# HGRN2 recurrence: near levels formed by groups of 32 tokens instead of whole blocks of 128

## The chip, the core and the metric

One Trainium2 chip, one core. The kernel computes a whole decoder layer in one launch, and the metric is its device time in microseconds (us). The tensor engine is called PE, its weight loads PEld, the vector engine DVE, the scalar engine ACT, GpSimd POOL; SP and ACT issue the DMAs.

## What is computed

A layer of width 2048 over 256 tokens: RMSNorm, one wide projection, two token mixers (block attention, and a gated linear recurrence), two gates that merge them, an output projection, and an MLP of 2048 to 8192 to 2048. The part that the change touches is the recurrence, with 8 heads, keys and values of 128:

```python
f = lb + (1 - lb) * sigmoid(f_pre);  k = 1 - f;  q = silu(q)
S_t = diag(f_t) S_{t-1} + k_t v_t^T          # state, 128 x 128 a head
o_t = S_t^T q_t
```

Unrolled, `o_t` is a sum over `s <= t` of `score[s, t] * v_s`, where `score[s, t]` sums over the 128 key dimensions `k_s * f_{s+1} * ... * f_t * q_t`. For `s = t` no decay stands between them.

## The kernel before

**The weight stream.** All products with weights go through "units" of 128x2048 float32, 1 MB each, loaded by SP in order (`load`), cut into two float32r parts, `hi` on ACT (line 116) and `lo` on DVE (line 117), two units ahead of their use (`cut`, `unit`, three buffers each of `raw`, `hi` and `lo`). A projection unit makes one 128x256 slice of the result: 16 products with `hi` and a moving operand of 512 columns (line 283, high and low part of the activation at once), and 16 with `lo` and 256 columns (line 285). The result leaves PSUM by ACT and DVE (`summed`, lines 296 and 297). Four PSUM banks hold such results.

**The work at the side.** Recurrence and attention are generators. After each unit, `step()` runs up to two of them for a budget of some us; each `yield` names an estimated cost. So PE's order is: one unit, a short burst of small products, the next unit, and so on. `recur(g, q, f)` handles four heads, for g = 0 and 1; it is started after the eight units that make its q and f.

**Scores by levels.** `recur` makes `score[s, t]` in a tile `sd` of 128 x 8 x 128: source token s on the partitions, 8 pairs of head h and block t of 128 tokens, target token in the row. The diagonal (line 339) is `ks^T q`, of which line 340 keeps the diagonal by a predicated copy with the mask `cmt`. Then level lv, with `h2 = 2**lv`, covers the pairs in which s lies in the left half and t in the right half of one group of `2*h2` tokens. The tiles `ks` and `qp` hold the decayed keys and queries for that level; DVE multiplies the next factors into them after each level (lines 392 to 395). For levels 0 to 4 one product a pair of head and block (line 361) takes all 128 keys as weights and the 64 right-half queries as the moving operand. It computes 128 x 64 scores, of which the mask keeps those inside a group (line 376). Levels 5 and 6 compute only what is needed, with weights of 32 or 64 keys (line 369): at level 5 the outputs go to partitions 0 to 31 and 64 to 95, at level 6 to partitions 0 to 63. ACT copies them to `sd` (line 384). Level 7 joins the two blocks (line 400). Lines 411 to 413 multiply the scores by the values.

These products are plain float32, and the trace shows two records for each, called passes here: level 5 has 16 products and 32 passes a burst; a level of 0 to 4, and the diagonal, 8 products and 16 passes.

**Constants.** `load_consts` issues three DMAs on SP after the fourth unit: `cft`, `rope` and `cmt`.

Of the kernel before, what the change touches and what calls it, by code (L numbers as in the profile page):

```python
# [11 lines left out]
I32 = mybir.dt.int32  # L12
AF = mybir.ActivationFunctionType
# [3 lines left out]
P = 128  # L17
# [13 lines left out]
def layer_kernel(ctx: ExitStack, tc: tile.TileContext, xT, vecs, wv, wm, wg, wu, wo, w1, w2, cf, cm, out):  # L31
    nc = tc.nc

    cp = ctx.enter_context(tc.tile_pool(name="const", bufs=1))
# [9 lines left out]
    def uid(s):  # L44
        cnt[0] += 1
        return f"{s}_{cnt[0]}"

    def g4(s, shape=(P, 1024), dt=F32):
        return gp.tile(list(shape), dt, tag="g", name=uid(s))

    def s1(s, dt=F32, n=256):
        return sp.tile([P, n], dt, tag=f"s{n}", name=uid(s), bufs=6 if n == 256 else 3)

    def bank(s, pool=pp):
        return pool.tile([P, 512], F32, tag="b", name=uid(s))
# [107 lines left out]
        load(u)  # L163
    cft = cp.tile([P, 128 + 256], F32, name="cft")
    rope = cp.tile([32, 512], F32, name="rope")
    cmt = cp.tile([P, 128 + 5 * 64], I32, name="cmt")

    def load_consts():
        nc.sync.dma_start(cft, cf[:, :384])
        nc.sync.dma_start(rope, cf[:32, 384:896])  # L170
        nc.sync.dma_start(cmt, cm)

    ident = cft[:, :128]
    cmask = cft[:, 128:384]
# [81 lines left out]
    for c in range(4):  # L256
        pst = [bank(f"pv{t}", pm) for t in range(2)]
        for q in range(4):
            hi, lo = unit()
            hi, lo = (x.rearrange("p (k f) -> p k f", k=4) for x in (hi, lo))  # L260
            for k in range(4):
                kk = 4 * q + k
                for t in range(2):
                    xh = xcat[:, kk, t * P : (t + 1) * P]
                    xl = xcat[:, kk, T + t * P : T + (t + 1) * P]
                    nc.tensor.matmul(pst[t], xh, hi[:, k, :], start=(kk == 0), stop=False)  # L266
                    nc.tensor.matmul(pst[t], xh, lo[:, k, :], start=False, stop=False)  # L267
                    nc.tensor.matmul(pst[t], xl, hi[:, k, :], start=False, stop=(kk == KD - 1))  # L268
            if c == 0 and q == 3:
                load_consts()  # L270
                side.append(prepare())
            step(3.6)
            if q == 3 and full:
                leave(*full.pop())
        full.append((c, pst))
# [42 lines left out]
    def recur(g, q, f):  # L318
        sg = g4("rsg", (P, 4, T))
        nc.scalar.activation(sg, q, AF.Sigmoid)  # L320
        nc.scalar.activation(f, f, AF.Sigmoid)
        nc.vector.tensor_mul(q, q, sg)
        yield 1.2
        for h in range(4):
            hh = 4 * g + h
            nc.vector.tensor_scalar(
                f[:, h, :], f[:, h, :], lb[:, 1, hh : hh + 1], lb[:, 0, hh : hh + 1], op0=OP.mult, op1=OP.add
            )
        ks = g4("rks", (P, 4, T))
        nc.vector.tensor_scalar(ks, f, -1.0, 1.0, op0=OP.mult, op1=OP.add)  # L330
        sd = g4("rsd", (P, 8, P))
        nc.gpsimd.memset(sd, 0.0)
        yield 1.5
        for b in range(2):
            pd = bank("pd")
            for i in range(4):
                h, t = divmod(4 * b + i, 2)
                c = slice(t * P, (t + 1) * P)
                nc.tensor.matmul(pd[:, i * P : (i + 1) * P], ks[:, h, c], q[:, h, c], start=True, stop=True)  # L339
            nc.vector.copy_predicated(  # L340
                sd[:, 4 * b : 4 * b + 4, :],
                cmt[:, None, :128].to_broadcast([P, 4, P]),
                pd.rearrange("p (a t) -> p a t", a=4),
            )
        qp = g4("rqp", (P, 4, T))
        nc.vector.tensor_mul(qp, q, f)
        yield 2.3
        sx = g4("rsx", (P, 4, P))
        tot = f.rearrange("p h t -> p (h t)")
        for lv in range(LEVELS):  # L350
            h2 = 1 << lv
            nb = P // (2 * h2)
            pd = bank("pd")
            if lv < 7:
                for h in range(4):
                    for t in range(2):
                        i = 2 * h + t
                        if lv < 5:
                            c = slice(t * P, (t + 1) * P)
                            rhs = qp[:, h, c].rearrange("p (n a j) -> p n a j", a=2, j=h2)[:, :, 1, :]  # L360
                            nc.tensor.matmul(  # L361
                                pd[:, i * 64 : (i + 1) * 64].rearrange("p (n j) -> p n j", j=h2),
                                ks[:, h, c], rhs, start=True, stop=True,
                            )
                            continue
                        for n in range(nb):
                            at = n * 2 * h2
                            c = t * P + at
                            nc.tensor.matmul(  # L369
                                pd[at : at + h2, i * h2 : (i + 1) * h2],  # L370
                                ks[:, h, c : c + h2], qp[:, h, c + h2 : c + 2 * h2], start=True, stop=True,
                            )
                if lv < 5:
                    mk = cmt[:, 128 + 64 * lv : 192 + 64 * lv].rearrange("p (n j) -> p n j", j=h2)
                    dst = sd.rearrange("p i (n a j) -> p i n a j", a=2, j=h2)[:, :, :, 1, :]
                    nc.vector.copy_predicated(
                        dst,
                        mk[:, None, :, :].to_broadcast([P, 8, nb, h2]),
                        pd.rearrange("p (i n j) -> p i n j", i=8, j=h2),
                    )  # L380
                else:
                    for n in range(nb):
                        at = n * 2 * h2
                        nc.scalar.activation(
                            sd[at : at + h2, :, at + h2 : at + 2 * h2],
                            pd[at : at + h2, : 8 * h2].rearrange("p (i j) -> p i j", i=8), AF.Copy,
                        )
                kv = ks.rearrange("p h (n a j) -> p (h n) a j", a=2, j=h2)
                qv = qp.rearrange("p h (n a j) -> p (h n) a j", a=2, j=h2)
                tv = tot.rearrange("p (n a) -> p n a", a=2)  # L390
                n = kv.shape[1]
                nc.vector.tensor_mul(kv[:, :, 0, :], kv[:, :, 0, :], tv[:, :, 1:2].to_broadcast([P, n, h2]))
                nc.vector.tensor_mul(qv[:, :, 1, :], qv[:, :, 1, :], tv[:, :, 0:1].to_broadcast([P, n, h2]))
                nt = sp.tile([P, n], F32, tag="tot" if n > 256 else "tots", name=uid("tot"), bufs=2)
                nc.vector.tensor_mul(nt, tv[:, :, 0], tv[:, :, 1])
                tot = nt
                yield 2.2
            else:
                for h in range(4):
                    nc.tensor.matmul(  # L400
                        pd[:, h * P : (h + 1) * P], ks[:, h, :P], qp[:, h, P:], start=True, stop=True
                    )
                nc.scalar.activation(sx, pd.rearrange("p (h t) -> p h t", h=4), AF.Copy)
                yield 0.1
        o = g4("ro", (P, 4, T))
        for b in range(2):
            po = bank("po")
            for j in range(2):
                h = 2 * b + j
                hc = slice((4 * g + h) * P, (4 * g + h + 1) * P)  # L410
                nc.tensor.matmul(po[:, j * T : j * T + P], ii[0][:, hc], sd[:, 2 * h, :], start=True, stop=True)
                nc.tensor.matmul(po[:, j * T + P : (j + 1) * T], ii[0][:, hc], sx[:, h, :], start=True, stop=False)
                nc.tensor.matmul(
                    po[:, j * T + P : (j + 1) * T], ii[1][:, hc], sd[:, 2 * h + 1, :], start=False, stop=True
                )
            nc.scalar.activation(o[:, 2 * b : 2 * b + 2, :], po.rearrange("p (h t) -> p h t", h=2), AF.Copy)
        ro[g] = o
        yield 0.1
# [111 lines left out]
    for g in range(2):  # L530
        q = g4("rq", (P, 4, T))
# [13 lines left out]
    for g in range(2):  # L545
        q = g4("aq", (P, 4, T))
# [17 lines left out]
    for j in range(KD):  # L564
# [8 lines left out]
        r = s1("r")  # L573
        summed(pr, r)
        nc.vector.tensor_mul(r, r, gr)
        a = s1("a")
# [10 lines left out]
    for c in range(4):  # L587
        t = g4("x2", (P, 4, T))
# [36 lines left out]
    for part in range(4):  # L625
        ucat = []
        for j in range(16):
# [5 lines left out]
            t = s1("t")  # L633
# [115 lines left out]
```

## Time and profile before

| what | us |
|---|---|
| median of 3 runs | 1441.9 (1441.51 to 1443.44) |
| profiled execution, its own time | 1443.69 |
| its span, first to last instruction | 1441.9 |
| PE busy in the span | 1435.0 |
| DVE, ACT, POOL busy | 881.5, 695.2, 4.4 |

The profile shows one execution. Busy times are shares of the span; an idle engine that nothing waits for costs nothing. What an edit is worth is read from the stage in which it lies.

### The profile page before, as it was taken

To read this page: it belongs to the slowest core of one execution; us is meant where nothing else is said; L and a number is where in the kernel's file an instruction comes from. 1 tells how busy PE (TensorE), PEld (TensorE's weight loads), DVE (VectorE), ACT (ScalarE), POOL (GpSimd) and SP (SyncE) were. 2 spreads that over 40 slices of the span, in tenths; PEclk is the share of its full clock that TensorE was granted. 3 is DMA by queue.
4 is the path that set the end of the run, shared out by engine and by line. 5 is a ranking of instruction groups with operands and counts; after the bars stand their busy time and mean duration, and the time that the engine had idled before them with its cause. 6 is when DMAs were issued, how large, how long until landed. Compare 5 with 4: busy or idle time off the path is not lost.

```text
span 1441.9 us, 18721 instructions
## 1 busy us (share of the span) xinstructions
PE 1435.0 (100%) x7824; PEld 1244.3 (86%) x7824; DVE 881.5 (61%) x958; ACT 695.2 (48%) x786; POOL 4.4 (0%) x10
## 2 busy tenths in 40 slices
PE   9999999999999999999999999999999999999998
PEld 7888989888888888888888888888888888888887
DVE  8445776667877667667666534555446555556553
ACT  7444443566764555545454443454335543354431
POOL 0000000000000000000000000000000000000000
PEclk9999999999999999999999999999999999999999
DMA  9555543445444455555555565555555555655571
GB/s 330 202 202 185 175 147 134 144 162 187 166 173 150 177 214 190 208 200 195 185 187 193 175 199 188 200 196 181 187 192 205 182 188 187 202 204 176 181 223 63
DMA packets 66324, 268.08 MB, mean 186 GB/s; under 512 B 4768, under 2 KB 7072, under 8 KB 43456
## 3 DMA queue, kind: packets, MB, share of 16 engines
q1 hardware_dynamic: 64368, 263.70, 53.7%
q0 software_dynamic: 576, 2.10, 0.4%
q8 instruction: 61, 1.00, 0.3%
q10 hardware_dynamic: 1296, 1.09, 0.2%
q14 instruction: 23, 0.19, 0.0%
HBM read 264.78 MB, written 2.10 MB: 185 GB/s over the span
## 4 chain that ended last, share of the span: by engine, by line
PE 99%; DMA 0%; DVE 0%; ACT 0%; issue 0%; DVEq 0%
PE pw L283 43%; PE pw L285 22%; PE py L651 8%; PE py L653 8%; PE py L652 8%; PE pv L266 2%; PE pv L267 2%; PE pv L268 2%; PE pd L361 1%; PE pl L489 0%; DMA vt<-vecs 0%; PE pt L620 0%; PE pd L339 0%; PE pd L369 0%; PE pb L433 0%; PE pb L434 0%
## 5 line engine op out<-in xcount | busy, mean ns | idle before, releaser
L117 DVE TENSOR_TENSOR lo<-raw,hi 128x2048 fp32r<-128x2048 f32 (+2 forms) x258 | 569.3, 2208 | 465.2 <-ACT hi L116 463.7
L116 ACT ACTIVATE hi<-raw 128x2048 fp32r<-128x2048 f32 (+2 forms) x258 | 475.6, 1845 | 462.7 <-PE pw L283 214.3
L283 PE MATMUL pw<-xcat,hi 128*128 128x512 f32 x1152 | 278.0, 393 | 0.0
L283 PEld LDWEIGHTS pw<-xcat,hi 128*128 128x128 f32 x1152 | 212.0, 188 | 42.1
L283 PE MATMUL pw<-x2cat,hi 128*128 128x512 f32 x1024 | 244.4, 391 | 0.0
L283 PEld LDWEIGHTS pw<-x2cat,hi 128*128 128x128 f32 x1024 | 188.4, 188 | 36.8 <-DVE x2cat L599 0.2
L651 PE MATMUL py<-hi,ucat 128*128 128x512 f32 x512 | 199.5, 390 | 0.0
L652 PE MATMUL py<-lo,ucat 128*128 128x512 f32 x512 | 199.2, 389 | 0.0
L653 PE MATMUL py<-hi,ucat 128*128 128x512 f32 x512 | 199.2, 389 | 0.0
L285 PEld LDWEIGHTS pw<-xcat,lo 128*128 128x128 f32 x1152 | 147.7, 191 | 5.6
L285 PE MATMUL pw<-xcat,lo 128*128 128x256 f32 x1152 | 149.4, 283 | 0.0
L285 PEld LDWEIGHTS pw<-x2cat,lo 128*128 128x128 f32 x1024 | 131.3, 191 | 4.9
L285 PE MATMUL pw<-x2cat,lo 128*128 128x256 f32 x1024 | 132.8, 283 | 0.0
L653 PEld LDWEIGHTS py<-hi,ucat 128*128 128x128 f32 x512 | 96.1, 188 | 20.0
L652 PEld LDWEIGHTS py<-lo,ucat 128*128 128x128 f32 x512 | 96.2, 188 | 19.7
L651 PEld LDWEIGHTS py<-hi,ucat 128*128 128x128 f32 x512 | 96.1, 188 | 19.7
L637 ACT ACTIVATE u<-t 128x256 f32<-128x256 f32 x64 | 26.4, 412 | 131.7 <-DVE t L635 131.7
L296 ACT ACTIVATE cross<-pw 128x256 f32<-128x256 f32 x168 | 62.3, 371 | 35.9 <-PE pw L285 35.8
L283 PE MATMUL pw<-mcat,hi 128*128 128x512 f32 x256 | 61.2, 391 | 0.0
L283 PEld LDWEIGHTS pw<-mcat,hi 128*128 128x128 f32 x256 | 47.0, 188 | 9.3 <-DVE mcat L310 0.3
L266 PE MATMUL pv<-hi,xcat 128*128 128x512 f32 x128 | 50.3, 400 | 1.4 <-ACT xcat L195 1.4
L267 PE MATMUL pv<-lo,xcat 128*128 128x512 f32 x128 | 50.5, 395 | 0.0
(170 smaller groups left out, 1027.8 us busy)
## 6 DMA issues: line engine op xcount, KB each, us to landing
raw<-w SPq DMA_DIRECT2D x128, 1024.0 KB, 5.3
raw<-wm SPq DMA_DIRECT2D x56, 1024.0 KB, 4.8
raw<-wg SPq DMA_DIRECT2D x16, 1024.0 KB, 4.8
raw<-wu SPq DMA_DIRECT2D x16, 1024.0 KB, 4.8
raw<-wo SPq DMA_DIRECT2D x16, 1024.0 KB, 4.9
raw<-wv SPq DMA_DIRECT2D x10, 1024.0 KB, 4.9
raw<-wv SPq DMA_DIRECT2D x8, 512.0 KB, 6.8
raw<-wv SPq DMA_DIRECT2D x8, 256.0 KB, 5.8
```

Of the source, the lines that this page charges most:

```text
L116: nc.scalar.activation(hi[:, s], raw[:, s], AF.Copy)
L117: nc.vector.tensor_sub(lo[:, s], raw[:, s], hi[:, s].bitcast(F32))
L266: nc.tensor.matmul(pst[t], xh, hi[:, k, :], start=(kk == 0), stop=False)
L267: nc.tensor.matmul(pst[t], xh, lo[:, k, :], start=False, stop=False)
L268: nc.tensor.matmul(pst[t], xl, hi[:, k, :], start=False, stop=(kk == KD - 1))
L283: nc.tensor.matmul(pst, h, cat, start=(i == 0), stop=False)
L285: nc.tensor.matmul(pst[:, T:], l, cat[:, :T], start=False, stop=(i == n - 1))
L296: nc.scalar.activation(c, pst[:, T:], AF.Copy)
L637: nc.scalar.activation(u2, t, AF.Square)
L651: nc.tensor.matmul(pst[t], uh, hi[:, k], start=(kk == 0), stop=False)
L652: nc.tensor.matmul(pst[t], uh, lo[:, k], start=False, stop=False)
L653: nc.tensor.matmul(pst[t], ul, hi[:, k], start=False, stop=(kk == 15))
```

## The change

The scores of the diagonal and of levels 0 to 4 all lie inside groups of 32 tokens. Before, they were computed for blocks of 128 keys and masked down. Now each block is split into four groups b of 32 tokens. A product takes the 32 keys of a group as weights and that group's queries as the moving operand (32 for the diagonal, 16 right-half ones for a level), and its output lies on partitions 32b to 32b+31. So there are four small products in place of each one. The scores are gathered in a new, packed tile `near` of 128 x 8 x 32, which POOL clears and DVE fills by predicated copies with packed masks. After level 4, four copies on ACT move it to `sd`. `near` takes one of the six buffers of 256 columns that the units' results use. The masks are loaded in eight small DMAs in place of one.

```diff
-        nc.sync.dma_start(cmt, cm)
+        for b in range(4):
+            r = slice(32 * b, 32 * b + 32)
+            nc.sync.dma_start(eye32[r], cm[r, 32 * b : 32 * b + 32])
+            m = cm[r, 128:].rearrange("p (v c) -> p v c", v=5)
+            nc.sync.dma_start(left[r], m[:, :, 16 * b : 16 * b + 16])
...
+        near = s1("near").rearrange("p (i t) -> p i t", i=8)
+        nc.gpsimd.memset(near, 0.0)
         yield 1.5
-        for b in range(2):
-            pd = bank("pd")
-            for i in range(4):
-                h, t = divmod(4 * b + i, 2)
-                c = slice(t * P, (t + 1) * P)
-                nc.tensor.matmul(pd[:, i * P : (i + 1) * P], ks[:, h, c], q[:, h, c], start=True, stop=True)
-            nc.vector.copy_predicated(
-                sd[:, 4 * b : 4 * b + 4, :],
-                cmt[:, None, :128].to_broadcast([P, 4, P]),
-                pd.rearrange("p (a t) -> p a t", a=4),
-            )
+        pd = bank("pd")
+        for h in range(4):
+            for t in range(2):
+                for b in range(4):
+                    c = slice(t * P + 32 * b, t * P + 32 * b + 32)
+                    i = 2 * h + t
+                    nc.tensor.matmul(
+                        pd[32 * b : 32 * b + 32, i * 32 : (i + 1) * 32], ks[:, h, c], q[:, h, c], start=True, stop=True
+                    )
+        nc.vector.copy_predicated(
+            near,
+            eye32[:, None, :].to_broadcast([P, 8, 32]),
+            pd[:, :256].rearrange("p (i t) -> p i t", i=8),
+        )
...
                         if lv < 5:
-                            c = slice(t * P, (t + 1) * P)
-                            rhs = qp[:, h, c].rearrange("p (n a j) -> p n a j", a=2, j=h2)[:, :, 1, :]
-                            nc.tensor.matmul(
-                                pd[:, i * 64 : (i + 1) * 64].rearrange("p (n j) -> p n j", j=h2),
-                                ks[:, h, c], rhs, start=True, stop=True,
-                            )
+                            for b in range(4):
+                                c = slice(t * P + 32 * b, t * P + 32 * b + 32)
+                                rhs = qp[:, h, c].rearrange("p (n a j) -> p n a j", a=2, j=h2)[:, :, 1, :]
+                                dst = pd[32 * b : 32 * b + 32, i * 16 : (i + 1) * 16]
+                                nc.tensor.matmul(
+                                    dst.rearrange("p (n j) -> p n j", j=h2), ks[:, h, c], rhs, start=True, stop=True
+                                )
                             continue
...
                 if lv < 5:
-                    mk = cmt[:, 128 + 64 * lv : 192 + 64 * lv].rearrange("p (n j) -> p n j", j=h2)
-                    dst = sd.rearrange("p i (n a j) -> p i n a j", a=2, j=h2)[:, :, :, 1, :]
+                    mk = left[:, lv, :].rearrange("p (n j) -> p n j", j=h2)
+                    dst = near.rearrange("p i (n a j) -> p i n a j", a=2, j=h2)[:, :, :, 1, :]
                     nc.vector.copy_predicated(
                         dst,
-                        mk[:, None, :, :].to_broadcast([P, 8, nb, h2]),
-                        pd.rearrange("p (i n j) -> p i n j", i=8, j=h2),
+                        mk[:, None, :, :].to_broadcast([P, 8, 16 // h2, h2]),
+                        pd[:, :128].rearrange("p (i n j) -> p i n j", i=8, j=h2),
                     )
+                    if lv == 4:
+                        for b in range(4):
+                            r = slice(32 * b, 32 * b + 32)
+                            nc.scalar.activation(sd[r, :, r], near[r], AF.Copy)
```

## Rows read from the trace of the kernel before

**Rows 1.** The page: span, busy time by engine.
```profile
span 1441.9 us, 18721 instructions
...
PE 1435.0 (100%) x7824; PEld 1244.3 (86%) x7824; DVE 881.5 (61%) x958; ACT 695.2 (48%) x786; POOL 4.4 (0%) x10
```

**Rows 2.** The recurrence's stage: busy PE, PEld, DVE, ACT, POOL; clock, DMA share, GB/s.
```profile
150.00:290.00 140.00, 140.00 (x964) 126.37 (x963) 99.85 (x131) 63.88 (x64) 0.00 (x0) 1.00 0.43 151
```

**Rows 3.** PE by shape, whole run: busy us, mean ns of one pass.
```profile
L361 PE MATMUL pd<-rqp,rks 128*128 128x64 f32 x160 | 19.0, 271 | 0.0
...
L369 PE MATMUL pd<-rqp,rks 128*64 128x64 f32 x32 | 2.3, 225 | 0.0
...
L369 PE MATMUL pd<-rqp,rks 128*32 128x32 f32 x64 | 1.4, 197 | 0.0
```

**Rows 4.** PE in order of time: start us, length us, work.
```profile
144.91 2.08 PE L285 MATMUL pw<-xcat,lo 128*128 128x256 f32 x16
...
150.48 2.08 PE L285 MATMUL pw<-xcat,lo 128*128 128x256 f32 x16
...
156.04 2.08 PE L285 MATMUL pw<-xcat,lo 128*128 128x256 f32 x16
...
163.42 2.08 PE L285 MATMUL pw<-xcat,lo 128*128 128x256 f32 x16
...
170.79 2.08 PE L285 MATMUL pw<-xcat,lo 128*128 128x256 f32 x16
172.71 1.90 PE L361 MATMUL pd<-rqp,rks 128*128 128x64 f32 x16
...
180.08 1.90 PE L361 MATMUL pd<-rqp,rks 128*128 128x64 f32 x16
```

**Rows 5.** The same view around levels 5 and 6 of the first four heads.
```profile
200.29 2.07 PE L285 MATMUL pw<-xcat,lo 128*128 128x256 f32 x16
202.29 0.70 PE L369 MATMUL pd<-rqp,rks 128*32 128x32 f32 x32
...
206.69 2.07 PE L285 MATMUL pw<-xcat,lo 128*128 128x256 f32 x16
208.69 1.15 PE L369 MATMUL pd<-rqp,rks 128*64 128x64 f32 x16
...
213.53 2.08 PE L285 MATMUL pw<-xcat,lo 128*128 128x256 f32 x16
```

**Rows 6.** Line 369's waits in PE's queue (first at 199.9); PEld's loads after that.
```profile
L369 PEldq EVENT_SEMAPHORE  x4: 51/51/51, 199.9 to 274.2; - x4
...
200.07 2.09 PEld L285 LDWEIGHTS pw<-xcat,lo 128*128 128x128 f32 x16
```

**Rows 7.** DVE in one period of the recurrence: first and last of six, and the copy.
```profile
172.96 2.29 DVE L117 TENSOR_TENSOR lo<-raw,hi 128x2048 fp32r<-128x2048 f32 x1 [2.08 <-ACT hi L116]
...
175.50 1.30 DVE L376 COPY_PREDICATED rsd<-cmt,pd 128x512 f32<-128x512 int32 x1
...
177.57 0.68 DVE L393 TENSOR_TENSOR rqp<-rqp,tot 128x512 f32<-128x512 f32 x1
```

**Rows 8.** By shape: DVE's predicated copies and ACT's copies into `sd`.
```profile
L376 DVE COPY_PREDICATED rsd<-cmt,pd 128x512 f32<-128x512 int32 x10 | 9.4, 945 | 0.0
...
L384 ACT ACTIVATE rsd<-pd 32x256 f32<-32x256 f32 x4 | 1.5, 374 | 0.6 <-PE pd L369 0.6
```

**Rows 9.** SP's queue around the constants; DVE's and PE's work on the next unit.
```profile
21.94 0.44 SPq L170 DMA_DIRECT2D rope<-cf  x1
22.42 1.12 SPq L171 DMA_DIRECT2D cmt<-cm  x1
25.61 11.32 SPq L94 DMA_DIRECT2D raw<-wv  x4
...
34.29 2.28 DVE L117 TENSOR_TENSOR lo<-raw,hi 128x2048 fp32r<-128x2048 f32 x1
...
41.42 0.39 PE L266 MATMUL pv<-hi,xcat 128*128 128x512 f32 x1
```

More of the change, by code (lines that the diff above doesn't have):

```diff
@@ L165, in layer_kernel @@
     rope = cp.tile([32, 512], F32, name="rope")
-    cmt = cp.tile([P, 128 + 5 * 64], I32, name="cmt")
+    eye32 = cp.tile([P, 32], I32, name="eye32")
+    left = cp.tile([P, 5, 16], I32, name="left")
     def load_consts():
```

## The prediction

> **What bounds the kernel now.** I read the page first: PE is busy for 1435.0 of a span of 1441.9 us, DVE for 61%, ACT for 48% [rows 1]. The table by stages asks whether that also holds where the recurrence runs: from 150 to 290 us PE is busy for all 140.00 us at a granted clock of 1.00, which is the 2.4 GHz level, DVE for 99.85, ACT for 63.88, and the DMA engines are 43% busy [rows 2]. So whatever PE does there is paid in full, and what DVE, ACT and the queues do is paid only where it makes PE wait. A change of PE's time counts us for us.
>
> Busy time is no price here, because passes overlap: 160 passes of line 361 have a mean length of 271 ns but only 19.0 us together [rows 3]. The price of a burst is read from the beat of the units, from one start of line 285 to the next. Without a burst the beat is 150.48 - 144.91 = 5.57 us. With the diagonal it is 163.42 - 156.04 = 7.38, with a level of line 361 it is 170.79 - 163.42 = 7.37 [rows 4]. So each of these bursts costs 1.80 us. There are twelve: five levels and a diagonal, for two groups of heads. They hold 21.6 us, 1.5% of the span, and that is the most that the change could take.
>
> **What sets the price of a burst.** Two other bursts show it. Level 5 costs 206.69 - 200.29 - 5.57 = 0.83 us, level 6 costs 213.53 - 206.69 - 5.57 = 1.27 us [rows 5]. The pace of passes is the burst's length, less its last pass, over the intervals. With 128 keys as weights: (1.90 - 0.27) / 15 = 109 ns. With 64: (1.15 - 0.22) / 15 = 62 ns. With 32, at level 5: (0.70 - 0.20) / 31 = 16 ns [rows 3 to 5]. Line 361's passes have the same 64 moving columns as level 6's, yet take nearly twice as long, so the number of weight columns sets the pace. A straight line through the first two gives 38 ns for 32 columns. Level 5 shows less than half of that. Its outputs alternate between two strips of 32 partitions; all those of level 6 lie on one strip of 64. I read this as two strips of the array working at once. What is left of a burst's cost after passes times pace is fixed: 1.80 - 16 x 0.109 = 0.06 us at full width, 1.27 - 16 x 0.062 = 0.28 at 64 columns, 0.83 - 32 x 0.016 = 0.32 at 32. Going to narrow products and back costs some 0.3 us.
>
> **The change part by part.** *PE.* Each of the twelve bursts has 8 x 4 = 32 products, two passes each, so 64 passes of 32 weight columns in place of 16 of 128. The diagonal's have level 5's exact shape; the levels' have 16 moving columns, which I price alike since the weights set the pace. Cost: 64 x pace + 0.32 us. The pace on four strips is not in the trace. Its bounds are 8 ns, if four strips halve what two show, and 38 ns, if the strips did nothing for each other. I take 10 ns, near the lower bound: the second strip cost nothing visible (16 is below half of 38), and 38 / 4 is 9.5. Then a burst costs 0.64 + 0.32 = 0.96 us, saves 0.84, and twelve save 10.1 us.
>
> A page of the Trainium skill has a measurement that bears on this pace. TensorE: Matmul & The Clock Gate, section Part 3: Packing small matmuls, gives a speedup of 2.38 for three column strips and 3.07 for four row strips; by the second, as an estimate, a single-strip pace of 38 ns would become 12, a burst 1.09 us, and the sum 8.5 us saved. No row here has four strips.
>
> *DVE.* A level's predicated copy shrinks from 512 to 128 elements a partition, from a mean of 0.945 us [rows 8]; the diagonal's two copies become one. That is nothing off the path by itself, but it shortens the chain that the next burst waits for. In the period shown, DVE's cut of a unit begins at 172.96, the level's copy at 175.50, and the last factor is in at 177.57 + 0.68 = 178.25, 1.83 us ahead of its burst at 180.08 [rows 4, 7]. Shorter bursts take 0.84 of that away, the shorter copy gives some back; about 1 us is left. Cost 0; if the cover went, PE would wait in that period for what is missing.
>
> *ACT.* Four copies after level 4, in each group: eight of a shape close to 32x256, 0.374 us each [rows 8], 3.0 us in all. ACT is idle more than half of the stage [rows 2]. Behind them in its queue stand the cut of a unit and a result's copy out of PSUM; the cut runs two units ahead, some 11 us, and four banks hold results. Cost 0. These copies wait for DVE, DVE's first copy waits for POOL's clearing of `near`; both stand a beat or more ahead of their reader. `near` keeps one of six small buffers for about seven beats, and a unit needs two; DVE and ACT have the time to give them back. Cost 0.
>
> *SP.* Eight small DMAs stand where one stood. Its issue took 1.12 us, the one before it 0.44. So eight take 3.5 to 9.0 us. The next unit's load went out at 25.61, with SP free from 23.54: it moves to between 25.9 and 31.4, by 0.3 to 5.8 us. Its `lo` part was ready at 34.29 + 2.28 = 36.57, and PE began that unit (the 49th product of line 266, eight a unit) at 41.42, so 4.85 us of cover [rows 9]. Cost 0; at the far end 1 us, once. The DMA share of 0.43 later leaves room to catch up [rows 2].
>
> **Sum.** -10.1 us. The profiled execution took 1443.7 us, 1.8 more than its span, so it would come to 1433.6; the median of the runs shown is 1441.9, which leaves **1431.8 us**.
>
> **The rivals.** *Two strips' pace.* The array might keep two strips busy and no more, since nothing wider is in the trace. Then 64 x 0.016 + 0.32 = 1.34 us a burst, 12 x 0.46 = 5.5 us saved, **1436.4 us**. Against it: nothing in level 5 says that two is a limit.
>
> *PE's queue runs dry.* When line 369's wait was passed at 199.9, sixteen products of line 285 were still to start [rows 6]; so PE's queue holds some sixteen passes that are ready. Level 5's 32 passes needed sixteen more to arrive within their 0.50 us. It proves one pass in 31 ns and no better. The new burst has 64 passes; 48 must arrive while it runs. At one in 31 ns they need 1.49 us, a burst costs 1.81, and nothing changes: **1442.0 us**. Everything between this and my forecast is open; for a faster queue speaks that level 5 shows no slowing.
> A rule of the Trainium skill speaks for such a floor: TensorE: Matmul & The Clock Gate, section Wait — 56ns, not 53.3ns?, has starts never closer than about 25 ns, however small the product. By it, a burst would cost 64 x 0.025 + 0.32 = 1.92 us and the total, as an estimate, 1443.3. Level 5's 16 ns a pass [rows 5] contradict it as an overall floor; the measurement decides.
>
> *Strips in turn: slower.* A product's two passes write the same strip, one behind the other, and only then comes the next strip. If with smaller operands and four strips PE worked them off one by one at half of level 6's 62 ns, 64 x 0.031 + 0.32 = 2.30 us a burst, 12 x 0.50 = 6.0 us lost, **1447.9 us**. It decides from a pace of (1.80 - 0.32) / 64 = 23 ns on. Against it: level 5 has the same order of passes and runs at 16.
>
> **How the numbers follow.** Half a chance for the forecast (a pace of 8 to 12 ns, 1430.3 to 1433.4), a quarter for about two strips' pace (12 to 19 ns), 0.15 for the dry queue (within 0.2% of before, 2.9 us, about what a measurement of this kernel can tell from no change), 0.06 for strips in turn, and 0.04 for a pace below 8 ns or a cheaper return to wide products. Faster: 0.50 + 0.25 + 0.04 = 0.79; same 0.15; slower 0.06. The range goes from 1429.0, just below the best pace, to 1439.0, where the gain of the two-strip case ends; it leaves out the last two cases and the tail of the fourth.
>
> **What the profile after would show.** The beat of the recurrence's units at 5.57 + 0.96 = 6.53 us in place of 7.37, with 64 passes of 128x16 a level in about 0.8 us; no longer idle time of PE at its bursts, and none near 41 us; DVE's copies short. Wrong would be: passes that start evenly every 16 ns (two strips) or that begin close together and slow down after about sixteen (the queue); beats longer than 7.4 us (strips in turn); a gap of PE ahead of line 266 (the constants).

## The result, and the profile after

| what | before | after |
|---|---|---|
| median of six runs, us | 1442.7 (1441.51 to 1443.44) | 1431.2 (1430.2 to 1432.35) |
| profiled execution, its own time, us | 1443.69 | 1432.35 |
| its span, us | 1441.9 | 1430.6 |

The ratio is 0.9922, with an interval of 0.9909 to 0.9935. Forecast were 1431.8 us and a gain of 10.1; the spans give a gain of 11.3. In the experiments below, the profiled execution of the first run with one strip at a time was disturbed (a granted clock of 0.753), so its time is left out and its beats are read from another execution.

The page after the change, its span and the busy time by engine:

```profile
span 1430.6 us, 19881 instructions
...
PE 1423.7 (100%) x8400; PEld 1231.1 (86%) x8400; DVE 873.0 (61%) x956; ACT 697.2 (49%) x794; POOL 4.9 (0%) x12
```

PE's busy time fell by 11.3 us and the span by the same 11.3 [rows 1], while PE has 576 records more. The table by stages, same columns as [rows 2]:

```profile
150.00:290.00 140.00, 140.00 (x1608) 123.39 (x1607) 98.55 (x134) 72.12 (x78) 1.21 (x2) 1.00 0.45 159
```

PE is busy without a gap and at the same clock as before. The stage is still PE's alone, so its beats are the price. PE in order of time, after (start us, length us, work; line 290 was 285, 347 is the diagonal, 373 the levels 0 to 4, 380 levels 5 and 6):

```profile
150.20 2.08 PE L290 MATMUL pw<-xcat,lo 128*128 128x256 f32 x16
...
155.76 2.07 PE L290 MATMUL pw<-xcat,lo 128*128 128x256 f32 x16
157.77 0.76 PE L347 MATMUL pd<-rq,rks 128*32 128x32 f32 x64
...
162.22 2.07 PE L290 MATMUL pw<-xcat,lo 128*128 128x256 f32 x16
164.22 0.74 PE L373 MATMUL pd<-rqp,rks 128*32 128x16 f32 x64
...
168.64 2.07 PE L290 MATMUL pw<-xcat,lo 128*128 128x256 f32 x16
...
177.07 0.74 PE L373 MATMUL pd<-rqp,rks 128*32 128x16 f32 x64
...
194.34 2.07 PE L290 MATMUL pw<-xcat,lo 128*128 128x256 f32 x16
...
200.73 2.07 PE L290 MATMUL pw<-xcat,lo 128*128 128x256 f32 x16
...
207.57 2.08 PE L290 MATMUL pw<-xcat,lo 128*128 128x256 f32 x16
```

The plain beat is 155.76 - 150.20 = 5.56 us, as before (5.57). With the diagonal it is 6.46, with a level 168.64 - 162.22 = 6.42, where [rows 4] had 7.38 and 7.37. Levels 5 and 6, which the change leaves alone, are the control: 6.39 and 6.84, where [rows 5] had 6.40 and 6.84. So a diagonal saves 0.92 us and a level 0.95: 2 x 0.92 + 10 x 0.95 = 11.3 us, all of the span's difference. On balance nothing else in the run has to be explained.

By shape, after (busy us, mean ns of one):

```profile
L373 PE MATMUL pd<-rqp,rks 128*32 128x16 f32 x640 | 7.4, 185 | 0.0
...
L347 PE MATMUL pd<-rq,rks 128*32 128x32 f32 x128 | 1.5, 199 | 0.0
...
L387 DVE COPY_PREDICATED near<-left,pd 128x128 f32<-128x128 int32 x10 | 3.4, 342 | 0.0
...
L395 ACT ACTIVATE rsd<-near 32x256 f32<-32x256 f32 x8 | 3.3, 416 | 3.3 <-DVE near L387 3.2
```

With the prediction's rule, the pace is (0.74 - 0.185) / 63 = 8.8 ns for a level and (0.76 - 0.199) / 63 = 8.9 for the diagonal. A level costs 6.42 - 5.56 = 0.86 us, so 0.86 - 64 x 0.0088 = 0.30 us is fixed. In the single records of the burst at 164.22 the first four passes start 6 to 7 ns apart and the fifth 33 ns later; from there the starts repeat at 7, 6, 7 and 12 ns, four passes in 32 ns. After some 34 passes they come in pairs, two in 17 ns.

Spans of single executions differ by some 2 us from the start of the kernel alone: the products of the second unit begin at 13.8 to 14.2 us in most profiles here, and at 11.7 and 11.8 in those of two experiments. Where less than that is at stake, the beats decide.

### The profile page after: what moved, and what is told of

It is laid out like the page before. It is cut to its first block, busy times and chain, and to the rows that moved or that the text cites. A ratio compares the mean times of both kernels' runs of the same rounds, so it can differ in the third digit from the quotient of the medians.

```text
span 1430.6 us, 19881 instructions
## 1 busy us (share of the span) xinstructions
PE 1423.7 (100%) x8400; PEld 1231.1 (86%) x8400; DVE 873.0 (61%) x956; ACT 697.2 (49%) x794; POOL 4.9 (0%) x12
## 4 chain that ended last, share of the span: by engine, by line
PE 99%; DMA 0%; DVE 0%; ACT 0%; issue 0%; DVEq 0%
PE pw L288 43%; PE pw L290 22%; PE py L667 8%; PE py L666 8%; PE py L668 8%; PE pv L271 2%; PE pv L272 2%; PE pv L273 2%; PE pd L373 0%; PE pl L504 0%; DMA vt<-vecs 0%; PE pt L635 0%; PE pd L380 0%; PE pb L448 0%; PE pb L449 0%; PE ptr L526 0%
```

## The experiments

The theory is that the four strips of 32 weight columns work at once, so that four passes take little longer than one. (A strip is both 32 columns of the array and the 32 partitions of PSUM that take their results; no run here separates the two.) Its rivals are that PE gained by the smaller operands alone, that two strips are all that work together, and that PE's queue sets the pace.

**One strip at a time.** Levels 0 to 4 have the same 64 passes, but all eight products of a strip come one after another.

```diff
+                if lv < 5:
+                    for b, h, t in ((b, h, t) for b in range(4) for h in range(4) for t in range(2)):
...
-                            for b in range(4):
```

> Levels 0 to 4 with the same 32 products a burst, but strip by strip: eight products in a row write the same 32 partitions. Theory (strips of the array work side by side, and a pass of 32 weight columns on one strip alone takes about half of level 6's 62 ns, 31 ns): a burst of 64 x 0.031 + 0.30 = 2.28 us in place of 0.86, ten of them, +14.2 us on the changed kernel, about 1445.4, slower than before. Rival (narrow weights alone make the passes short, the strip doesn't matter): the beat stays at 6.43 us and the time at 1431.

> The same kernel as the first experiment, for its trace: a pace near the 28.7 ns a pass that its time suggests, (1443.5 - 1431.2) / 10 bursts = 1.23 us more each, so 1.23 + 0.86 - 0.30 = 1.79 us over 64 passes, 28 ns; a beat of 5.57 + 2.09 = 7.66 us. Rival (some bursts are held by waits and others not): beats that differ between levels.

The median was 1443.4 us, the ratio to the kernel before 1.0004 (0.9995 to 1.0013). PE in order of time, from the second run (1443.9 us):

```profile
162.10 2.07 PE L290 MATMUL pw<-xcat,lo 128*128 128x256 f32 x16
164.11 1.90 PE L371 MATMUL pd<-rqp,rks 128*32 128x16 f32 x64
...
169.70 2.07 PE L290 MATMUL pw<-xcat,lo 128*128 128x256 f32 x16
```

A level's beat is 7.60 us, alike at all levels, its cost 2.03, its pace (1.90 - 0.185) / 63 = 27.2 ns. Within a strip, passes start 32 ns apart in the single records; where one strip ends and the next begins, they come in twos for a few passes, which brings the mean down. That is why the time stayed 2 us below the expected 1445.4, which counts 31 ns for every pass. The same products in another order cost more than the wide ones did (1.80), and the whole gain of the levels is gone. So for the levels the smaller operands bring nothing by themselves; the order over strips brings it all.

**Two strips at a time.** Strips 0 and 1 alternate, then strips 2 and 3.

```diff
+                if lv < 5:
+                    for h, t, b in ((h, t, b) for p in range(2) for h in range(4) for t in range(2) for b in (2 * p, 2 * p + 1)):
...
-                            for b in range(4):
```

> Levels 0 to 4 with the products ordered so that first strips 0 and 1 alternate, then strips 2 and 3. Theory (as many products run at once as strips alternate): level 5's pace of 16 ns, a burst of 64 x 0.016 + 0.30 = 1.32 us, ten bursts, +4.6 us, about 1435.8. Rival (two strips are all the array overlaps, and 8.8 ns has another cause, such as the 16 moving columns): no change, 1431.

The median was 1435.7 us (ratio 0.9952, 0.9939 to 0.9966). PE in order of time:

```profile
162.26 2.07 PE L290 MATMUL pw<-xcat,lo 128*128 128x256 f32 x16
164.26 1.10 PE L371 MATMUL pd<-rqp,rks 128*32 128x16 f32 x64
...
169.05 2.07 PE L290 MATMUL pw<-xcat,lo 128*128 128x256 f32 x16
```

The beat is 6.79 us, the cost 1.23, the pace (1.10 - 0.185) / 63 = 14.5 ns. With one, two and four strips the pace is 27.2, 14.5 and 8.8 ns: it follows the number of strips, a little less than in proportion. The first two figures are lowered by the passes where the strips change. In the single records, one strip starts a pass every 32 ns, two strips start two passes in 32 ns, and four strips four, until the pairs of 17 ns set in. This is also what the rival of two strips would have looked like, and it forecast 1436.4 us for it, with the diagonal at that pace too.

**Every product twice.** The burst of a level gets 128 passes, the second half repeating the first.

```diff
+                if lv < 5:
+                    for h, t, b in 2 * [(h, t, b) for h in range(4) for t in range(2) for b in range(4)]:
...
-                            for b in range(4):
```

> Every product of levels 0 to 4 is issued twice in its burst, with the same output: 128 passes in place of 64. Theory (PE's queue is refilled at about the pace that the second half of the changed kernel's bursts shows, 8.5 ns a pass): +64 x 0.0085 = 0.54 us a burst, ten bursts, +5.4 us, about 1436.7. Rival (what stood ready in the queue carried the burst, and past it a pass comes every 31 ns): a burst of about 3.8 us, +29 us, about 1460.

The median was 1438.6 us (ratio 0.9971, 0.9960 to 0.9982). PE in order of time:

```profile
160.34 2.07 PE L290 MATMUL pw<-xcat,lo 128*128 128x256 f32 x16
162.34 1.27 PE L371 MATMUL pd<-rqp,rks 128*32 128x16 f32 x128
...
167.30 2.07 PE L290 MATMUL pw<-xcat,lo 128*128 128x256 f32 x16
...
244.94 2.07 PE L290 MATMUL pw<-xcat,lo 128*128 128x256 f32 x16
...
249.17 0.26 PE L371 MATMUL pd<-rqp,rks 128*32 128x16 f32 x8 [1.02 <-issue]
...
253.13 2.07 PE L290 MATMUL pw<-xcat,lo 128*128 128x256 f32 x16
```

The beat is 6.96 us, 0.54 above that of 64 passes: the second 64 cost 8.4 ns each and nothing fixed. The pace over the burst is (1.27 - 0.185) / 127 = 8.5 ns and stays there to its end. A queue that ran dry would have slowed the later passes to the prediction's 31 ns; after about the 34th pass they slow from 8 to 8.5 ns and no further. Ten such beats are 5.4 us. One burst out of ten also stood still for 1.02 us ahead of its last eight passes, with nothing in the profile that it waited for; its beat is 253.13 - 244.94 = 8.19 us, 1.2 more than its like. That makes 6.6; the medians differ by 7.4, of which the rest lies within the scatter of about 1 us either way.

**Each product again with half of its keys.** Instead of the repetition, a second pass over the same products with the first 16 of the 32 keys as weights. This is to tell apart what sets the 8.5 ns: a strip's own work, which half as many weight columns should shorten, or something common to all passes.

```diff
+                    for k, h, t, b in ((k, h, t, b) for k in (32, 16) for h in range(4) for t in range(2) for b in range(4)):
...
+                        dst = pd[32 * b : 32 * b + k, i * 16 : (i + 1) * 16]
...
+                            dst.rearrange("p (n j) -> p n j", j=h2), ks[:, h, c][:, :k], rhs, start=True, stop=True
```

> As the run with every product of levels 0 to 4 twice, but the second time with the first 16 keys of each group as weights: 128 passes a burst, half of them of 16 weight columns, same outputs. Theory (past its first third a burst runs at the pace at which passes reach the array, about 8.5 ns each whatever their width): the beat is the 6.97 us of the run with full products twice. Rival (the strips' own work sets the pace; on the line through 109 and 58 ns at 128 and 64 columns a pass of 16 columns takes 18 ns, on four strips 4.6): 64 x 0.008 + 64 x 0.0046 + 0.30 = 1.11 us, a beat of 6.67.

One run, 1438.8 us. PE in order of time:

```profile
162.29 2.07 PE L290 MATMUL pw<-xcat,lo 128*128 128x256 f32 x16
164.29 1.25 PE L371 MATMUL pd<-rqp,rks 128*32 128x16 f32 x128
...
169.23 2.07 PE L290 MATMUL pw<-xcat,lo 128*128 128x256 f32 x16
...
248.75 1.18 PE L371 MATMUL pd<-rqp,rks 128*32 128x16 f32 x120
250.99 0.23 PE L371 MATMUL pd<-rqp,rks 128*16 128x16 f32 x8 [1.06 <-issue]
```

The beat is 6.94 us, the repetition's length: passes with half as many weight columns come no faster, though each of their weight loads takes 93 ns in the records in place of 110. If 16 columns keep a strip for less time than 32, as the paces of 109, 62 and 32 ns for 128, 64 and 32 columns on one strip suggest, then past the first passes of a burst the four strips aren't the limit. No run has 16 columns on one strip alone, so this is argued and not shown. (The line through 109 and 58 ns gives 20 ns for 16 columns and not the 18 of the expectation; the rival's beat would then be about 6.69.) I read the two passes in 17 ns as the rate at which PE is given passes; no view shows this directly. The standstill of some 1 us came back after the 120th pass of level 3 of the second group, the same place as with the repetition. It belongs to the longer program at that place; what PE waited for was not found.

**The work at the side three times.** Each predicated copy of a level and each of the copies from `near` is issued three times.

```diff
-                    nc.vector.copy_predicated(
+                    for _ in range(3):
+                        nc.vector.copy_predicated(
...
-                        for b in range(4):
+                        for b in 3 * [0, 1, 2, 3]:
```

> The predicated copies of levels 0 to 4 are each done three times, and the four copies of ACT after level 4 too; PE's work is that of the changed kernel. Theory (work of DVE and ACT is covered: a level's wait is passed 1.85 us ahead of its burst, and two more copies of 0.34 us use 0.7 of that): no change, 1431 within 0.1%. Rival (the chain over DVE binds): PE waits 0.5 us or more a level, +5 us or more.

The median was 1432.2 us (ratio 0.9928, 0.9916 to 0.9941). The copies by shape (busy us, mean ns of one):

```profile
L388 DVE COPY_PREDICATED near<-left,pd 128x128 f32<-128x128 int32 x30 | 10.4, 347 | 0.0
...
L396 ACT ACTIVATE rsd<-near 32x256 f32<-32x256 f32 x24 | 9.9, 414 | 0.5
```

PE in order of time, in the same kernel:

```profile
160.26 2.07 PE L290 MATMUL pw<-xcat,lo 128*128 128x256 f32 x16
...
166.69 2.07 PE L290 MATMUL pw<-xcat,lo 128*128 128x256 f32 x16
```

DVE has 7.0 and ACT 6.6 us more to do, and the beat stays at 6.43. What the copies cost, once or three times, is hidden, so their shortening is no part of the gain.

**The masks in one DMA.** The constant input is laid out beforehand as the two mask tiles, so that one DMA brings both.

```diff
-    eye32 = cp.tile([P, 32], I32, name="eye32")
-    left = cp.tile([P, 5, 16], I32, name="left")
+    masks = cp.tile([P, 112], I32, name="masks")
...
+        nc.sync.dma_start(masks, cm)
```

> The changed kernel with its masks laid out packed beforehand and loaded in one DMA in place of eight. Theory (the eight DMAs only use up cover): the unit load behind them goes out near 25.6 us in place of 29.26, the parts of the following units are ready earlier, PE's order of work and the time stay as they are: 1431 within 0.1%. Rival (the late load holds PE somewhere): faster by more than 1 us.

The median was 1432.2 us (ratio 0.9925, 0.9911 to 0.9938). SP's queue in the changed kernel, with the first of the eight mask DMAs, the last, and the next unit's load:

```profile
22.58 0.42 SPq L174 DMA_DIRECT2D eye<-cm  x1
...
28.74 0.42 SPq L176 DMA_DIRECT2D left<-cm  x1
29.26 9.55 SPq L94 DMA_DIRECT2D raw<-wv  x4
```

The same view with the masks in one DMA:

```profile
21.80 0.42 SPq L173 DMA_DIRECT2D masks<-cm  x1
24.96 15.53 SPq L94 DMA_DIRECT2D raw<-wv  x5
```

In the changed kernel the eight DMAs occupy SP from 22.58 to 29.16, 6.6 us, and the next unit's load goes out at 29.26, where [rows 9] had 25.61. With one DMA it goes out at 24.96. The time is the same. DVE's `lo` parts of the two units that follow show what the delay used up, in the changed kernel:

```profile
36.16 2.29 DVE L117 TENSOR_TENSOR lo<-raw,hi 128x2048 fp32r<-128x2048 f32 x1 [1.70 <-ACT hi L116]
...
43.78 2.29 DVE L117 TENSOR_TENSOR lo<-raw,hi 128x2048 fp32r<-128x2048 f32 x1 [1.64 <-ACT hi L116]
```

The first is ready at 38.45, and PE begins that unit at 41.84: 3.4 us of cover. The second is ready at 46.07 for a start at 47.51: 1.4 us, where the trace of before has it ready at 40.42 for 47.56, 7.1 us. The second one lost more than the DMAs explain. In the changed kernel six passes that sum up the norm (lines 234 and 237) stand one unit earlier in PE's order. An operation of ACT waits 4.26 us for them, and behind it in ACT's queue stands that unit's `hi`. With one DMA they stand where they stood, and that part is ready at 40.13. So the constants cost nothing, with 1.4 us to spare.

**The diagonal and level 0 in one burst.** `q * f` is made a step earlier, so that both bursts follow one another without wide products between. The diagonal's predicated copy then comes after level 0's products.

```diff
-        yield 1.5
+        qp = g4("rqp", (P, 4, T))
+        nc.vector.tensor_mul(qp, q, f)
+        yield 2.7
...
-        yield 2.3
+        pdiag = pd
```

> The diagonal and level 0 share a burst (q*f is made a step earlier, so the products don't wait for DVE). Theory (each burst of narrow products pays some 0.30 us once, whatever it holds): 128 passes x 0.0086 + 0.30 = 1.40 us in place of 0.89 + 0.86 = 1.75, two such bursts, 0.7 us saved on the changed kernel: about 1430.5, too little for the times, to be read from a beat of 6.97 us in place of 6.45 and 6.43. Rival (the 0.30 us belong to the passes): the two bursts' sum, a beat of 7.31.

The median was 1431.7 us (ratio 0.9920, 0.9903 to 0.9938), not to be told from the changed kernel by the times. PE's beat of the merged burst:

```profile
156.00 2.07 PE L290 MATMUL pw<-xcat,lo 128*128 128x256 f32 x16
...
163.00 2.07 PE L290 MATMUL pw<-xcat,lo 128*128 128x256 f32 x16
```

It is 7.00 us for 128 passes, where the two separate bursts cost 0.90 + 0.86 above the plain beat. The merged one costs 1.44, so 0.32 is saved: the fixed 0.30 us is paid once a burst, not once a product.

**Levels 5 and 6 side by side.** Before and after the change, these use half of the array's columns at a time. Here the second block's products go to the idle strips, and ACT's copies put the result on its partitions.

```diff
-                                pd[at : at + h2, i * h2 : (i + 1) * h2],
+                                pd[at + h2 * t : at + h2 * t + h2, h * h2 : (h + 1) * h2],
...
+                        for t in range(2):
+                            nc.scalar.activation(
+                                sd.rearrange("p (h t) s -> p h t s", t=2)[at : at + h2, :, t, at + h2 : at + 2 * h2],
+                                pd[at + h2 * t : at + h2 * t + h2, : 4 * h2].rearrange("p (h j) -> p h j", h=4), AF.Copy,
+                            )
```

> Levels 5 and 6 put the second block's products on the strips that lie idle (32 to 63 and 96 to 127 at level 5, 64 to 127 at level 6); ACT copies them back across partitions, in twice as many copies of half the size. Theory (strips work side by side): level 5's 32 passes at 8.5 in place of 16 ns, beat 6.14 in place of 6.39; level 6's 16 passes at 29 in place of 58 ns, beat 6.34 in place of 6.84; together 1.5 us less, about 1429.7. Rival (64 wide strips don't overlap): level 6's beat stays at 6.84 and 0.5 us is saved.

The median was 1430.8 us (ratio 0.9916, 0.9900 to 0.9931). PE in order of time:

```profile
194.35 2.07 PE L290 MATMUL pw<-xcat,lo 128*128 128x256 f32 x16
196.36 0.46 PE L380 MATMUL pd<-rqp,rks 128*32 128x32 f32 x32
...
200.51 2.07 PE L290 MATMUL pw<-xcat,lo 128*128 128x256 f32 x16
202.51 0.69 PE L380 MATMUL pd<-rqp,rks 128*64 128x64 f32 x16
...
206.89 2.08 PE L290 MATMUL pw<-xcat,lo 128*128 128x256 f32 x16
```

Level 5's beat falls from 6.39 to 6.16 us, level 6's from 6.84 to 6.38, 0.7 us a group of heads and 1.4 in all. The medians differ by 0.4 us, too little to tell; the spans of the profiled executions differ by the 1.4 (1429.2 against 1430.6). Level 5's pace goes from 16 to (0.46 - 0.20) / 31 = 8.4 ns, level 6's from 62 to (0.69 - 0.225) / 15 = 31 ns. That is the theory shown a third time, on products that the change did not touch.

**Both together.** The last two edits in one kernel.

> The one burst for diagonal and level 0, and levels 5 and 6 with their blocks side by side. Theory: 0.7 + 1.5 us less than the changed kernel, about 1429.0. Rival (ACT's added copies or DVE's chain now hold PE): no gain or a loss against 1431.

The median was 1429.5 us (ratio 0.9909, 0.9893 to 0.9925), the lowest of all. It lies 1.7 us below the changed kernel, which the intervals don't separate; the beats of the two edits are there as in the single runs (7.01 us for the merged burst, 6.38 for level 6), except for one of 6.68 us at level 1 of the second group, 0.25 above its like. There PE's weight loads paused for 0.19 us among the wide products ahead of the burst, with nothing in the profile that they waited for.

## Why the prediction was right

**What bounds the kernel.** That a change of PE's beats counts us for us held to 0.1 us: 11.3 us from the beats, 11.3 from the spans. It was luck that the time came out nearer (0.6 us) than the gain (1.2 us): the forecast started from 1441.9, the median of three runs, and that of six is 1442.7.

**The pace.** 10 ns was taken, between 8 and 38; it is 8.8. The argument, that the second strip of level 5 cost nothing visible and two more would not either, is what the runs with one, two and four strips show. The pace of one strip alone was put at 38 ns by a straight line through wider weights; it is 32 within a strip. A quarter of that is 8, the lower bound, and the first passes of a burst run at it; then the 8.5 ns of the repetition takes over. The Trainium skill, TensorE: Matmul & The Clock Gate, section Part 3: Packing small matmuls, gives 3.07 for four row strips and 2.38 for three column strips. The trace agrees in size: 27.2 / 8.8 = 3.1 for four column strips and 27.2 / 14.5 = 1.9 for two. That 3.1 lies so near 3.07 is partly chance, since 27.2 is lowered where strips change; from the 32 ns within a strip the gain of four is 3.6.

**The fixed cost.** 0.32 us was taken from level 5, and 0.30 was measured. The gain was short by 12 x 64 x 0.0012 = 0.9 us for the pace and 12 x 0.02 = 0.2 for the fixed cost, 1.1 of the 1.2 us by which it was off.

**Costs of nothing.** DVE's and ACT's copies cost nothing even three times over. DVE's cover was mis-sized. "About 1 us is left" of 1.83, said the prediction. DVE in the changed kernel, in the period of the same level as [rows 7]:

```profile
170.81 2.29 DVE L117 TENSOR_TENSOR lo<-raw,hi 128x2048 fp32r<-128x2048 f32 x1 [2.01 <-ACT hi L116]
...
173.35 0.43 DVE L387 COPY_PREDICATED near<-left,pd 128x128 f32<-128x128 int32 x1
...
174.55 0.68 DVE L408 TENSOR_TENSOR rqp<-rqp,tot 128x512 f32<-128x512 f32 x1
```

The last factor is in at 175.23 and its burst begins at 177.07: 1.84 us. The copy went from 1.30 to 0.43 us and gave back nearly all of the 0.95 that the shorter beat took, where the prediction counted only "some". At the next level, where the copy had taken 0.70 us, the cover fell from 2.35 to 1.89. The constants went as foreseen: the load at 29.26 lies inside 25.9 to 31.4, and the cover of 4.85 us fell to 3.4. Not foreseen was that the order of PE's products changes with the number of DMAs, and that the unit after it is left with 1.4.

**The rivals.** *Two strips' pace* has its own kernel, 14.5 ns and 1435.7 us; the change isn't it. *PE's queue runs dry* is refuted at its price: 31 ns a pass was only what level 5 could prove, and 128 passes run at 8.5. Something of the kind may be there all the same, for the starts change from four in 32 ns to two in 17, and the 8.5 ns is the same for 32 and 16 weight columns. But they change after about the 34th pass and not after the sixteenth, which the prediction had read from [rows 6]. Level 5's 32 passes end before that place, so nothing in the trace of before could show the later pace; that it is no worse than 8.5 ns was luck. The Trainium skill, TensorE: Matmul & The Clock Gate, section Wait — 56ns, not 53.3ns?, has starts never closer than about 25 ns. The trace does not agree: passes on different strips start 6 to 12 ns apart. *Strips in turn* was priced at 31 ns and 2.30 us a burst; in the kernel that works strip by strip, it is 27 ns and 2.03 us. Its mechanism exists, but needs that order; a product's two passes on one strip don't bring it about, since the next strip doesn't wait for them.

## What to carry to other kernels

Price small products by the beat of the work around them, not by their busy time: 64 passes of 185 ns took 0.86 us, and the same 64 in another order 2.03. When products are cut narrow, put neighbours of the stream on different strips; narrow products that stay on one strip are no cheaper than the wide ones (1443.4 us against 1442.2 before), and half-used columns elsewhere (levels 5 and 6) are the next place to look. A change into narrow products and back costs 0.3 us, so bursts that can stand together should, and small DMAs on a queue that feeds the bound engine are to be counted against its cover.

## What the runs showed of the hardware

Starts of passes on four strips 6 to 12 ns apart, and a steady two in 17 ns later in the burst, independent of whether 32 or 16 weight columns are loaded, were not expected. Nor was a standstill of 1.0 us inside two longer bursts, at the same place of the program in two kernels; its cause is open. A candidate that no run tested is the fetching of instructions: its DMA queue moved 71 packets in the run with every product twice, and 66 in the changed kernel. SP needed 6.6 us for eight DMAs of 4 and 10 KB, each issued in 0.3 to 1.3 us, with pauses between some of them (24.41 to 25.38, 25.69 to 26.93) that no view explains.
